# Hybrid SSD and attention step: scan filler in half items, one sample state per step, state products over 128 rows

## Chip, core and metric

The kernel runs on one core of one Trainium2 chip. The metric is the device time of one execution in microseconds (us), the median of several runs; lower is better. A profile is one further execution, recorded instruction by instruction.

## What is computed

One inference step of a two-layer decoder: 512 prompt tokens of one sequence and 8 sample sequences of 8 tokens each (576 tokens in all) share the weights. Layer 0 mixes tokens with a Mamba-2 state scan, layer 1 with sliding-window attention; each layer has a SwiGLU feed-forward block before and after its mixer. The part that matters here is the scan of layer 0, with 4 groups (G) of 8 heads (R) of 64 features (P) and a state of 128 (N):

```python
def ssd_mixer(h, conv_buf, h0, in_w, conv_w, conv_b, dt_bias, a_log, d_skip, norm_w, out_w):
    zxbcdt = h @ in_w
    ...
    xbc = jax.nn.silu(causal_dwconv(xpad, conv_w, conv_b, l))
    ...
    y, h_T = ssd_scan(xdt, dt * A, Bm, Cm, h0.reshape(bsz, SSM_GROUPS, SSM_HPG, SSM_HEAD_DIM, SSM_STATE))
    y = y + xs * d_skip.reshape(SSM_GROUPS, SSM_HPG, 1)
    yg = (y.reshape(bsz, l, SSM_D_INNER) * jax.nn.silu(z)).astype(jnp.float32).reshape(bsz, l, SSM_GROUPS, -1)
    yg = yg * lax.rsqrt(jnp.mean(yg * yg, axis=-1, keepdims=True) + RMS_EPS)
    ...
    return yn @ out_w, new_conv, new_h

# inside ssd_scan, per chunk of at most 128 tokens
    chunk_states = jnp.einsum('bclgn,bclgrp->bcgrpn', Bc, xc * decay_to_end[..., None])
    def step(hc, inp):
        s, a = inp
        return hc * a[..., None, None] + s, hc
    y_off = jnp.einsum('bclgn,cbgrpn->bclgrp', Cc, h_in) * jnp.exp(a_cs)[..., None]
```

For the 8 sample sequences there is one chunk of 8 tokens each: read the old state, add its part to y, and write old state times decay plus the product of B and the decayed inputs.

## The kernel before

Activations lie with features on the partitions and tokens along the free axis, 576 of them in two token halves `HALF`: 256 and 320 columns. A projection block is a product of a 1024 x 128 weight with all tokens. Weights and activations are each split into a high and a low part, and `gemm` (line 501) issues three matmuls for each of 8 slices of the contraction, 24 a half. `load_w` loads a block on SP's queue (tile `raw`, two buffers), ScalarE (ACT) casts the high part `whi`, VectorE (DVE) subtracts the low part `wlo`. All matmuls of `gemm` stand as `g<-...` in the rows.

The scan, in `ssd`, goes through the four groups in turn. `mix` is a generator: it issues a step of a group's scan and yields, nine times in a group: the transposes and products of B and C (`bcs`); four prompt chunks (`chunk`); the within-chunk part of the samples and `old(0)`; `new(0)`; `old(1)`; `new(1)`. Each `old` reads the states of four samples (tile `h0`, four buffers; it is `h` in the trace), loaded on SP's queue, into products `pos` with 32 weight columns each, and a transpose `yot`. Each `new` multiplies the four states by their decay on GpSimd (POOL, line 1013), forms two products `psts` for each sample (line 1009 with the high part `xh` of the inputs, line 1010 with the low part `xl`), adds on DVE (line 1016) and stores on ACT's queue. A state buffer of the first four samples is free for a load of the second four only when its store has landed. In the 64 rows of `xl` lie the low parts; `xh` has 128 rows.

Between steps the caller issues filling work from a list: projections of the next group (`nxt`, six items: B, C and four x blocks, each followed by a convolution on DVE, line 863), the gate projections of this group (`zs`, four) and the output projections of the group before (`outs`, four loads of two feature blocks). An item holds both token halves. After step k of nine, `nfill * (k + 1) / 9` items have been issued. After step `GK` = 6 the gated product of the first token half is issued (`gate_mul`: `y` times z, squares, sums in `gacc`), after the next step its sum over the features (`gate_sum`: a matmul `gsq` on TensorE). The last `NG` items lie between the parts of the gated norm, `GB` of them ahead of the second `gate_sum`, `GC` behind it.

The engines run their queues in order. The order inside a queue is set when the kernel is built: a scheduler takes instructions as its own estimate of times lets them become ready, so it differs from the order of the code.

Of the kernel before, what the change touches and what calls it, by code (L numbers as in the profile page):

```python
# [10 lines left out]
F32 = mybir.dt.float32  # L11
F32R = mybir.dt.float32r
AF = mybir.ActivationFunctionType
ALU = mybir.AluOpType
# [5 lines left out]
HALF = ((0, 256), (256, 320))  # L20
# [19 lines left out]
FS = 0  # L40
NPRE = 4
PSP = 512
NX = 1
NG = 2
GK = 6
GJ = 2
GA = 0
GB = 1
GC = 1
FP = (0, 2)  # L50
N2 = T // 2
# [7 lines left out]
def body(ctx: ExitStack, tc: tile.TileContext, A, O):  # L59
# [421 lines left out]
    def gemm(w, acts, n, w0=0):  # L481

        return gemms([w], acts, n, w0)[0]
# [21 lines left out]
    def hin_acts(hin, h):  # L505
        return [(hin[h][:, 0, k, :], hin[h][:, 1, k, :]) for k in range(8)]
# [10 lines left out]
    def run_in(hin, items, first, ex, pend, between=None, pre=()):  # L517

        bd = last.pop() if first and last else None
        base = len(mms)  # L520
        ws = [bd.nextw[i] if bd and i < len(bd.nextw) else pre[i][0] if i < len(pre) else
              load_w(src, 1024, ex if i >= WR else None)
              for i, (src, _) in enumerate(items[:first])]
        if bd:
            bd.update(1)
            bd.close()
        for h in (0, 1):
            if between and h:
                between()
            for i, (w, (_, use)) in enumerate(zip(ws, items)):  # L530
                if h == 0 and i < len(pre):
                    use(h, gemm_part(w, hin_acts(hin, h), HALF[h][1], range(4, 8), pre[i][1]))
                else:
                    use(h, gemm(w, hin_acts(hin, h), HALF[h][1]))
            if bd and h == 0:
                bd.place(1, base)
        for src, use in items[first:]:
            w = load_w(src, 1024)
            for h in (0, 1):
                use(h, gemm(w, hin_acts(hin, h), HALF[h][1]))  # L540
            pend.step()
# [227 lines left out]
    def ssd(l, hin, f, pend, bd):  # L769
        with ExitStack() as cx:  # L770
# [122 lines left out]
            def mix(g, d, y, sa, se, dtt, cd):  # L893
# [111 lines left out]
                def new(q, xh, xl):  # L1005

                    for b in range(q * 4, q * 4 + 4):
                        pst = ps_s.tile([128, 512], F32, tag="s", name="psts")
                        PE.matmul(out=pst, lhsT=bm[:, b, :], rhs=xh, start=True, stop=False)
                        PE.matmul(out=pst, lhsT=bm[0:64, b, :], rhs=xl, start=False, stop=True)  # L1010
                        h0 = h0s.pop(b)
                        hv = h0.rearrange("p (h q) -> p h q", q=64)
                        G.tensor_tensor(out=hv, in0=hv,
                                        in1=cd[:, g * 8:g * 8 + 8, 4 + b].unsqueeze(2).to_broadcast([128, 8, 64]),
                                        op=ALU.mult)
                        V.tensor_tensor(out=h0, in0=pst, in1=h0, op=ALU.add)
                        nc.scalar.dma_start(O["ssm_s"][g, :, b], h0)

                for i in range(5):
                    bcs(i)  # L1020
                yield
                h = None
                for i in range(4):
                    h = chunk(i, h)
                    yield
                skip(slice(0, NP))
                xd, pyv = within(4)
                old(0)
                yield
                xh = R2.tile([128, 512], F32R, tag="xdd", name="xh", bufs=2)  # L1030
                xl = R2.tile([64, 512], F32R, tag="xl", name="xl", bufs=1)
                S.copy(xh, xd)
                V.tensor_tensor(out=xl, in0=xd[0:64], in1=xh[0:64].bitcast(F32), op=ALU.subtract)
                new(0, xh, xl)
                yield
                old(1)
                yv = y[:, :, NP:T]
                V.tensor_tensor(out=yv, in0=pyv, in1=yv, op=ALU.add)
                skip(slice(NP, T))
                yield  # L1040
                new(1, xh, xl)
                yield

            def z_item(g, j, zt):

# [55 lines left out]

            R = tc.tile_pool(name="ssdr", bufs=1, reuse_waits="tile")
            Rcm, R = R, R.__enter__()
            def run1(item):
                run_in(hin, [item()], 0, None, pend)

            d, items = proj_items(0)
            v = R.tile([96, T], F32, tag="xs", name="dtv", bufs=6)
# [10 lines left out]
            for g in range(4):  # L1119
                last = g == 3  # L1120
                fill = []
                outs = [lambda ld=ld, yn=yn: run_out([ld], yn_acts(yn), f, g == 1) for ld in out_loads(g - 1)] if g else []
                zt, ynew = [], []

                def z_run(j):
# [6 lines left out]
                    run1(lambda: z_item(g, j, zt[j]))  # L1132

                zs = [lambda j=j: z_run(j) for j in range(4)]
                dn, nxt = proj_items(g + 1) if not last else (None, [])
                nxt = [lambda it=it: run1(it) for it in nxt]
                fill = zs + outs if last else nxt[:NX] + outs + zs + nxt[NX:]
                nfill = len(fill) - NG

                y = R.tile([128, 4, T], F32, tag="y", name="y", bufs=1)  # L1140
                steps = mix(g, d, y, *dd)
                done = 0
                for k, _ in enumerate(steps):
                    while done < nfill * (k + 1) / 9:
                        fill.pop(0)()
                        done += 1
                    if k == GK:
                        acc = gate_mul(0, y, zt)
                    if k == GK + 1:
                        r0 = gate_sum(0, acc)  # L1150
                fl = iter(fill)
                run = lambda c: [next(fl, lambda: None)() for _ in range(c)]
                acc = gate_mul(1, y, zt)
                ynew += [yn_alloc() for _ in range(4)]
                run(GA)
                gate_norm(0, g, y, bcast(r0, HALF[0][1]), ynew)
                run(GB)
                r1 = gate_sum(1, acc)
                run(GC)
                gate_norm(1, g, y, bcast(r1, HALF[1][1]), ynew)  # L1160
                run(len(fill))
                yn, d = ynew, dn
# [523 lines left out]
```

## Time and profile before

| what | value |
|---|---|
| time, median of 3 runs | 2581.92 us (2581.41 to 2588.04) |
| the profiled execution's own time | 2593.07 us |
| span of its profile, first to last instruction | 2591.0 us |
| TensorE (PE) matmul busy | 2493.8 us, 96% |
| VectorE busy | 1804.0 us, 70% |
| ScalarE busy | 1152.3 us, 44% |
| GpSimd busy | 202.8 us, 8% |
| mean granted TensorE clock | 0.977 |

The profiled execution took 11 us longer than the median. Busy times come from the record of each instruction; a matmul's end is modelled, so for TensorE the spacing of starts tells more than the busy share. In a timeline row the bracket at the end is the idle time of that engine just before the row, and what ended it. The scan runs from about 556 us to 995 us of the span. A 32-bit matmul that is not split stands as two records.

### The profile page before, as it was taken

Reading aid. Unit: us, or ns where it says so; the run is one execution under the profiler, and the core shown is the slowest. Engines: PE = TensorE matmul, PEld = TensorE weight load, DVE = VectorE, ACT = ScalarE, POOL = GpSimd, SP = SyncE. Lnnn points to the kernel's source line nnn. Section 1 sums busy time; section 2 is a strip of 40 time slices with the busy share of each in tenths; the row PEclk is TensorE's granted clock in tenths of the full one; section 3 lists DMA queues with packets and bytes.
Section 4 is the critical chain, followed back from the end, with each engine's and each line's share of the span. In section 5 each row is a group of like instructions: output and inputs, shape, how many; then the busy total and the mean of one; then the engine's idle time right before and its main releaser. Section 6 shows DMA issues by size and latency. Waiting matters only on the chain.

```text
span 2591.0 us, 45688 instructions
## 1 busy us (share of the span) xinstructions
PE 2493.8 (96%) x18247; PEld 2309.2 (89%) x18247; DVE 1804.0 (70%) x3415; ACT 1152.3 (44%) x2396; POOL 202.8 (8%) x338
## 2 busy tenths in 40 slices
PE   6999999989999999999999999999999998999997
PEld 5999998877989878899999999999899788999997
DVE  5576766887768686667767757675766756577685
ACT  4343434554645454334424534342454664343343
POOL 1000000123131312000000100000010001000001
PEclk8999999999999999899999999999999998999998
DMA  7344534244444342344333343443436123233222
GB/s 261 106 167 135 191 134 167 94 117 130 122 131 107 131 115 107 120 138 127 122 135 120 121 139 107 167 177 126 168 124 202 34 70 107 94 101 103 91 94 110
DMA packets 119499, 331.04 MB, mean 128 GB/s; under 512 B 17903, under 2 KB 39903, under 8 KB 108671
## 3 DMA queue, kind: packets, MB, share of 16 engines
q1 hardware_dynamic: 100535, 245.46, 29.3%
q10 hardware_dynamic: 18752, 82.68, 9.3%
q8 instruction: 143, 2.34, 0.4%
q14 instruction: 69, 0.57, 0.1%
HBM read 301.63 MB, written 29.67 MB: 128 GB/s over the span
## 4 chain that ended last, share of the span: by engine, by line
PE 80%; DVE 8%; DMA 4%; ACT 3%; issue 3%; POOL 1%; SPq 0%; DVEq 0%; ACTq 0%; POOLq 0%
PE g L501 40%; PE g L673 29%; PE adaps L164 2%; DMA w<-scr_a 1%; PE gram L343 1%; DVE wlo L472 1%; DVE acc L863 1%; DMA raw<-in_w_out 1%; PE po L1298 1%; DVE hin L439 1%; PE py L947 1%; PE ssq L234 1%; DVE pn L436 1%; PE rb L255 1%; DMA x<-x_dram 1%
## 5 line engine op out<-in xcount | busy, mean ns | idle before, releaser
L501 PE MATMUL g<-hin,whi 128*128 128x320 f32 (+1 forms) x2528 | 533.4, 304 | 1.8 <-DVE hin L439 1.8
L501 PE MATMUL g<-mid,whi 128*128 128x320 f32 (+1 forms) x2432 | 489.3, 296 | 0.0
L673 PE MATMUL g<-hin,whi 128*128 128x288 f32 x2176 | 436.2, 294 | 0.0
L501 PEld LDWEIGHTS g<-hin,whi 128*128 128x128 f32 x2528 | 418.6, 194 | 10.3 <-issue 6.6
L501 PE MATMUL g<-hin,wlo 128*128 128x320 f32 (+1 forms) x1264 | 388.1, 309 | 16.1 <-ACT sil L724 7.0
L501 PEld LDWEIGHTS g<-mid,whi 128*128 128x128 f32 x2432 | 390.7, 188 | 1.1
L501 PE MATMUL g<-mid,wlo 128*128 128x256 f32 (+1 forms) x1216 | 359.8, 297 | 2.4 <-ACT mid L685 2.2
L673 PEld LDWEIGHTS g<-hin,whi 128*128 128x128 f32 x2176 | 349.1, 188 | 0.0
L673 PE MATMUL g<-tcmb,whi 128*128 128x288 f32 x1632 | 327.2, 294 | 0.0
L673 PE MATMUL g<-hin,wlo 128*128 128x288 f32 x1088 | 324.2, 298 | 0.0
L469 ACT CAST whi<-raw 128x1024 fp32r<-128x1024 f32 (+2 forms) x209 | 188.0, 900 | 236.3 <-PE g L501 162.5
L472 DVE TENSOR_TENSOR wlo<-raw,whi 128x1024 fp32r<-128x1024 f32 (+3 forms) x209 | 216.4, 1038 | 85.7 <-ACT whi L469 84.7
L501 PEld LDWEIGHTS g<-hin,wlo 128*128 128x128 f32 x1264 | 244.3, 194 | 33.7 <-issue 11.0
L673 PEld LDWEIGHTS g<-tcmb,whi 128*128 128x128 f32 x1632 | 262.5, 189 | 0.0
L673 PE MATMUL g<-tcmb,wlo 128*128 128x288 f32 x816 | 245.5, 301 | 0.0
L501 PEld LDWEIGHTS g<-mid,wlo 128*128 128x128 f32 x1216 | 228.6, 188 | 7.1 <-ACT mid L685 4.6
L652 ACT CAST whi<-scmb 128x512 fp32r<-128x512 f32 (+1 forms) x204 | 154.3, 760 | 160.8 <-PE g L673 83.5
L673 PEld LDWEIGHTS g<-hin,wlo 128*128 128x128 f32 x1088 | 204.1, 188 | 23.9 <-issue 23.9
L566 DVE TENSOR_TENSOR f<-g,f 128x256 f32<-128x256 f32 (+1 forms) x240 | 108.6, 455 | 143.4 <-PE g L501 142.2
L648 DVE TENSOR_TENSOR wlo<-scmb,whi 128x512 fp32r<-128x512 f32 (+1 forms) x204 | 175.6, 863 | 36.1 <-ACT whi L652 35.2
L673 PEld LDWEIGHTS g<-tcmb,wlo 128*128 128x128 f32 x816 | 153.3, 188 | 25.1 <-DVE ur L648 19.7
L652 ACT CAST whi<-raw 128x512 fp32r<-128x512 f32 x136 | 84.7, 623 | 166.2 <-PE g L673 98.4
(299 smaller groups left out, 3898.9 us busy)
## 6 DMA issues: line engine op xcount, KB each, us to landing
adaw<-in_ada_w ACTq DMA_DIRECT2D x56, 1024.0 KB, 5.4
raw<-in_w_in SPq DMA_DIRECT2D x108, 512.0 KB, 3.5
rawu<-in_w_in SPq DMA_DIRECT2D x68, 512.0 KB, 4.5
raw<-in_w_out SPq DMA_DIRECT2D x64, 384.0 KB, 3.1
raw<-in_w_out SPq DMA_DIRECT2D x64, 320.0 KB, 3.0
raw<-in_w_ssm SPq DMA_DIRECT2D x40, 512.0 KB, 3.5
x_dram<-x SPq DMA_DIRECT2D x10, 1024.0 KB, 3.9
x<-x_dram SPq DMA_DIRECT2D x10, 1024.0 KB, 6.3
```

The source lines that it names most:

```text
L164: PE.matmul(out=pt[32 * j:32 * j + 32, :w], lhsT=cs[:, k, :], rhs=aw[:, j * w:j * w + w], start=(k == 0), stop=(k == 7))
L234: ins = PE.matmul(out=ps[:, c0 + i:c0 + i + 1], lhsT=acc[:, o:o + 128], rhs=ones[:, 0:1], start=True, stop=True)
L255: ins = PE.matmul(out=r[:, c:e], lhsT=mul(y[:, i:i + 1], [128, 128]), rhs=ident[:, 128 - (e - c):128], start=True, stop=True)
L343: ins = PE.matmul(out=out, lhsT=a, rhs=b, start=(o == i == 0), stop=(o == 7), skip_group_check=True)
L436: V.scalar_tensor_tensor(out=tm, in0=x_cur[h][:, k, :], scalar=mv["gs"][:, k, 0:1], in1=r[:, :256], op0=ALU.mult, op1=ALU.mult)
L469: S.copy(hi[:, :n], raw[:, :n])
L472: i = (V if early and c < PSP else eng or V).tensor_tensor(out=lo[:, c:e], in0=raw[:, c:e], in1=hi[:, c:e].bitcast(F32), op=ALU.subtract)
L501: mms.append(PE.matmul(out=p[:, :n], lhsT=wt[:, a:b], rhs=at, start=(k == j == 0), stop=(j == 2 and k == K - 1)))
L566: V.tensor_tensor(out=fs, in0=p, in1=fs, op=ALU.add)
L648: e.tensor_tensor(out=out, in0=a, in1=b, op=op)
L652: S.copy(w[0][:, c:c + n], src)
L673: mms.append(PE.matmul(out=p, lhsT=wt[:, o], rhs=x, start=(first and k == j == 0), stop=(k == 3 and j == 2), skip_group_check=True))
```

## The change

The filling list now holds pieces: a projection item is two pieces, one for each token half (`pieces`), and an output load is two pieces, one for each feature block with both halves (`out_pieces`). The counts double with them (`NX` 1 to 2, `NG` 2 to 4); `GB` goes from one item to three pieces, `GC` stays at one, now a piece. `mix` yields after each sample of `new`, with weights that add to 36; pieces are issued up to `nfill * k / 36`. The gated product of the first half follows at k = 28 and its sum at k = 32, the same places of `mix` as before. The low part `xl` now has 128 rows, of which the upper 64 are set to zero on DVE, and the second product of a state takes all 128 rows of `bm`.

```diff
-NX = 1
-NG = 2
-GK = 6
+NX = 2
+NG = 4
...
-GB = 1
+GB = 3
...
-                        PE.matmul(out=pst, lhsT=bm[0:64, b, :], rhs=xl, start=False, stop=True)
+                        PE.matmul(out=pst, lhsT=bm[:, b, :], rhs=xl, start=False, stop=True)
...
                         nc.scalar.dma_start(O["ssm_s"][g, :, b], h0)
+                        yield 1
...
-                xl = R2.tile([64, 512], F32R, tag="xl", name="xl", bufs=1)
+                xl = R2.tile([128, 512], F32R, tag="xl", name="xl", bufs=1)
+                V.memset(xl[64:128].bitcast(F32), 0.0)
                 S.copy(xh, xd)
-                V.tensor_tensor(out=xl, in0=xd[0:64], in1=xh[0:64].bitcast(F32), op=ALU.subtract)
-                new(0, xh, xl)
-                yield
+                V.tensor_tensor(out=xl[0:64], in0=xd[0:64], in1=xh[0:64].bitcast(F32), op=ALU.subtract)
+                yield from new(0, xh, xl)
...
+            def pieces(item):
+
+                got = {}
+
+                def half(h):
+                    if h == 0:
+                        src, got["use"] = item()
+                        got["w"] = load_w(src, 1024)
+                    got["use"](h, gemm(got["w"], hin_acts(hin, h), HALF[h][1]))
+                    if h:
+                        pend.step()
+
+                return [lambda h=h: half(h) for h in (0, 1)]
+
+            def out_pieces(ld, yn, first):
...
+                def one(i):
+                    if i == 0:
+                        got["w"] = load_w(src, n)
+                    o, w0 = os_[i]
+                    for h in (0, 1):
+                        p = gemm(got["w"], yn_acts(yn)(h), HALF[h][1], w0)
...
-                done = 0
-                for k, _ in enumerate(steps):
-                    while done < nfill * (k + 1) / 9:
+                done = k = 0
+                for part in steps:
+                    k += part
+                    while done < nfill * k / 36:
                         fill.pop(0)()
                         done += 1
-                    if k == GK:
+                    if k == 28:
                         acc = gate_mul(0, y, zt)
-                    if k == GK + 1:
+                    if k == 32:
                         r0 = gate_sum(0, acc)
```

The order moves in all four groups from the sample part of the first on. Three places follow, all in the second group (group 1), where the kernel before has its pattern of the middle groups. One removed line of constants makes the line numbers ahead of the inserted code smaller by one after the change.

TensorE, the first four state products of group 1, before (the number after `psts` tells one sample from the next; `g` is filling work):

```order
L1009 MATMUL psts_8040<-xh_8036,bm_7235 128x512
L1010 MATMUL psts_8040<-xl_8037,bm_7235 128x512
L1009 MATMUL psts_8046<-xh_8036,bm_7235 128x512
L1010 MATMUL psts_8046<-xl_8037,bm_7235 128x512
L1009 MATMUL psts_8052<-xh_8036,bm_7235 128x512
L1010 MATMUL psts_8052<-xl_8037,bm_7235 128x512
L501 MATMUL g_8071<-hin_5193,wlo_8068 128x256
...
L1009 MATMUL psts_8058<-xh_8036,bm_7235 128x512
L1010 MATMUL psts_8058<-xl_8037,bm_7235 128x512
```

The same place after:

```order
L1008 MATMUL psts_8042<-xh_8037,bm_7236 128x512
L1009 MATMUL psts_8042<-xl_8038,bm_7236 128x512
L500 MATMUL g_8055<-hin_5193,wlo_8052 128x256
...
L1008 MATMUL psts_8083<-xh_8037,bm_7236 128x512
L1009 MATMUL psts_8083<-xl_8038,bm_7236 128x512
L500 MATMUL g_8089<-hin_5193,wlo_8052 128x320
...
L1008 MATMUL psts_8117<-xh_8037,bm_7236 128x512
L1009 MATMUL psts_8117<-xl_8038,bm_7236 128x512
L1008 MATMUL psts_8123<-xh_8037,bm_7236 128x512
L1009 MATMUL psts_8123<-xl_8038,bm_7236 128x512
```

A whole token half of filling work (24 matmuls) now stands behind the first product pair and another behind the second.

TensorE, the four state reads of `old(1)` of group 1 up to the transpose `yot`, before:

```order
L994 MATMUL pos_8232<-h0_8233,C_6621 32x512
L994 MATMUL pos_8232<-h0_8235,C_6621 32x512
L994 MATMUL pos_8232<-h0_8237,C_6621 32x512
L994 MATMUL pos_8232<-h0_8239,C_6621 32x512
L501 MATMUL g_8266<-hin_5193,wlo_8263 128x256
...
L1000 MATMUL yot_8247<-c_ident_89,yo_8245 128x128 x4
```

and after:

```order
L993 MATMUL pos_8190<-h0_8191,C_6621 32x512
L993 MATMUL pos_8190<-h0_8193,C_6621 32x512
L500 MATMUL g_8216<-hin_5193,wlo_8135 128x320
...
L993 MATMUL pos_8190<-h0_8195,C_6621 32x512
L500 MATMUL g_8216<-hin_5193,wlo_8135 128x320
L500 MATMUL g_8216<-hin_5193,whi_8134 128x320 x2
...
L993 MATMUL pos_8190<-h0_8197,C_6621 32x512
L500 MATMUL g_8268<-hin_5193,wlo_8265 128x256
...
L999 MATMUL yot_8205<-c_ident_89,yo_8203 128x128 x4
```

The four reads stood together and are now a pair and two single ones, with filling work between; 24 filling matmuls stand between the fourth state product and the first read, where 92 stood.

DVE of group 1, from the convolution of C to the sums of squares of the first token half (`gacc`), which the matmul `gsq` reads; before:

```order
L863 SCALAR_TENSOR_TENSOR acc<-xpt,c_convw,acc 128x64
L1003 TENSOR_TENSOR y<-yot,y 128x4x32
L472 TENSOR_TENSOR wlo<-raw,whi 128x1024
L870 SCALAR_TENSOR_TENSOR C<-th,acc 128x320
L1038 TENSOR_TENSOR y<-py,y 128x4x64
L953 SCALAR_TENSOR_TENSOR y<-xs,c_dsk,y 128x64 x4
L1066 TENSOR_TENSOR gacc<-gacc,sq 128x256
L1060 SCALAR_TENSOR_TENSOR y<-y,z 128x320
```

and after:

```order
L862 SCALAR_TENSOR_TENSOR acc<-xpt,c_convw,acc 128x256 x3
L869 SCALAR_TENSOR_TENSOR C<-th,acc 128x256
L1065 TENSOR_TENSOR gacc<-gacc,sq 128x256 x2
L862 SCALAR_TENSOR_TENSOR acc<-xpt,c_convw,acc 128x256 x2
L862 SCALAR_TENSOR_TENSOR acc<-xpt,c_convw,acc 128x64
...
L1002 TENSOR_TENSOR y<-yot,y 128x4x32
```

The sums now stand ahead of the second half of C's convolution and of the work behind `yot`; before they stood behind both.

## Rows read from the trace of the kernel before

**Rows 1.** The page: TensorE's granted clock in 40 slices, and the chain.

```profile
PEclk8999999999999999899999999999999998999998
PE 80%; DVE 8%; DMA 4%; ACT 3%; issue 3%; POOL 1%; SPq 0%; DVEq 0%; ACTq 0%; POOLq 0%
```

**Rows 2.** TensorE's waits from 556 to 995 us: total, times, longest.

```profile
PE gsq L234 <- DVE gacc L1066: 7.5, 6, 2.8
PE py L947 <- DVE w L943: 3.1, 7, 1.1
```

**Rows 3.** Windows: PE, PEld, DVE, ACT, POOL busy, clock, DMA share, GB/s.

```profile
700.00:740.00 40.00, 40.00 (x291) 34.89 (x291) 22.90 (x38) 12.55 (x28) 6.30 (x7) 1.00 0.42 133
740.00:775.00 35.00, 32.22 (x205) 28.20 (x204) 27.81 (x58) 19.88 (x51) 13.43 (x27) 0.90 0.38 118
865.00:900.00 35.00, 32.22 (x192) 27.42 (x191) 25.55 (x53) 18.70 (x47) 11.72 (x24) 0.85 0.37 122
```

**Rows 4.** The state products' tile: duration min/median/max in ns, first and last start.

```profile
L1009 PE MATMUL psts<-xh,bm x32: 388/502/794, 610.8 to 984.9; 128*128 128x512 f32 x32
L1010 PE MATMUL psts<-xl,bm x32: 491/500/792, 611.1 to 985.3; 64*128 64x512 f32 x32
```

**Rows 5.** Timeline of weight loads, first four state products: start, length, idle before.

```profile
611.50 0.19 PEld L1009 LDWEIGHTS psts<-xh,bm 128*128 128x128 f32 x1 [0.24 <-issue]
611.93 0.18 PEld L1010 LDWEIGHTS psts<-xl,bm 64*128 64x128 f32 x1 [0.24 <-issue]
612.36 0.19 PEld L1009 LDWEIGHTS psts<-xh,bm 128*128 128x128 f32 x1 [0.24 <-issue]
```

**Rows 6.** Timeline of matmuls, filling work at full clock.

```profile
720.21 0.28 PE L501 MATMUL g<-hin,wlo 128*128 128x256 f32 x1
...
720.57 0.31 PE L501 MATMUL g<-hin,wlo 128*128 128x320 f32 x1
...
721.01 0.31 PE L501 MATMUL g<-hin,wlo 128*128 128x320 f32 x1
```

**Rows 7.** Timeline of matmuls, first gated sum of groups 1 and 2.

```profile
751.29 0.61 PE L234 MATMUL gsq<-c_ones,gacc 128*128 128x1 f32 x4 [2.78 <-DVE gacc L1066]
...
757.72 0.41 PE L501 MATMUL g<-hin,wlo 128*128 128x256 f32 x1
...
758.36 0.41 PE L501 MATMUL g<-hin,wlo 128*128 128x256 f32 x1
...
879.90 1.01 PE L234 MATMUL gsq<-c_ones,gacc 128*128 128x1 f32 x4 [2.78 <-DVE gacc L1066]
```

**Rows 8.** Timeline of DVE and POOL ahead of that sum.

```profile
741.60 5.10 DVE L863 SCALAR_TENSOR_TENSOR acc<-xpt,c_convw,acc 128x256 f32<-128x256 f32 x6 [1.13 <-ACT acc L860]
...
750.82 0.41 DVE L1066 TENSOR_TENSOR gacc<-gacc,sq 128x256 f32<-128x256 f32 x1
...
741.53 4.49 POOL L1013 TENSOR_TENSOR h<-h,cd 128x512 f32<-128x512 f32 x4 [0.26 <-PE pos L994]
```

**Rows 9.** Timeline of matmuls around state reads: four together, then a single one.

```profile
740.01 0.46 PE L501 MATMUL g<-hin,whi 128*128 128x320 f32 x2
...
741.40 0.39 PE L501 MATMUL g<-hin,wlo 128*128 128x256 f32 x1
...
973.18 0.28 PE L501 MATMUL g<-yn,whi 128*128 128x256 f32 x1
...
974.36 0.38 PE L501 MATMUL g<-yn,whi 128*128 128x256 f32 x1
```

**Rows 10.** State stores and loads (KB, us to landing), and a read that waits.

```profile
h<-in_h SPq DMA_DIRECT2D x32, 256.0 KB, 4.2
out_ssm_s<-h ACTq DMA_DIRECT2D x32, 256.0 KB, 2.1
...
621.94 1.05 PE L994 MATMUL pos<-h,C 128*32 128x512 f32 x2 [0.23 <-DMA h<-in_h]
```

**Rows 11.** The low part's tile: duration min/median/max in ns.

```profile
L1033 DVE TENSOR_TENSOR xl<-xdd,xh x4: 784/802/1204, 605.8 to 961.4; 64x512 fp32r<-64x512 f32 x4
```

More of the change, by code (lines that the diff above doesn't have):

```diff
@@ L1017, in new @@
                         nc.scalar.dma_start(O["ssm_s"][g, :, b], h0)
+                        yield 1
                 for i in range(5):
                     bcs(i)
-                yield
+                yield 4
                 h = None
@@ L1024, in mix @@
                     h = chunk(i, h)
-                    yield
+                    yield 4
                 skip(slice(0, NP))
@@ L1028, in mix @@
                 old(0)
-                yield
+                yield 4
                 xh = R2.tile([128, 512], F32R, tag="xdd", name="xh", bufs=2)
-                xl = R2.tile([64, 512], F32R, tag="xl", name="xl", bufs=1)
+                xl = R2.tile([128, 512], F32R, tag="xl", name="xl", bufs=1)
+                V.memset(xl[64:128].bitcast(F32), 0.0)
                 S.copy(xh, xd)
-                V.tensor_tensor(out=xl, in0=xd[0:64], in1=xh[0:64].bitcast(F32), op=ALU.subtract)
-                new(0, xh, xl)
-                yield
+                V.tensor_tensor(out=xl[0:64], in0=xd[0:64], in1=xh[0:64].bitcast(F32), op=ALU.subtract)
+                yield from new(0, xh, xl)
                 old(1)
@@ L1039, in mix @@
                 skip(slice(NP, T))
-                yield
-                new(1, xh, xl)
-                yield
+                yield 4
+                yield from new(1, xh, xl)
             def z_item(g, j, zt):
@@ L1103, in ssd @@
             Rcm, R = R, R.__enter__()
+            def pieces(item):
[9 more added lines that the diff above has]
+            def out_pieces(ld, yn, first):
+                src, n, os_ = ld
+                got = {}
+                def one(i):
[4 more added lines that the diff above has]
+                        p = gemm(got["w"], yn_acts(yn)(h), HALF[h][1], w0)
+                        if first:
+                            S.copy(f[h][:, o, :], p)
+                        else:
+                            V.tensor_tensor(out=f[h][:, o, :], in0=p, in1=f[h][:, o, :], op=ALU.add)
+                return [lambda i=i: one(i) for i in range(len(os_))]
             def run1(item):
-                run_in(hin, [item()], 0, None, pend)
+                for piece in pieces(item):
+                    piece()
             d, items = proj_items(0)
@@ L1121, in ssd, with z_make @@
                 fill = []
-                outs = [lambda ld=ld, yn=yn: run_out([ld], yn_acts(yn), f, g == 1) for ld in out_loads(g - 1)] if g else []
+                outs = [p for ld in out_loads(g - 1) for p in out_pieces(ld, yn, g == 1)] if g else []
                 zt, ynew = [], []
-                def z_run(j):
+                def z_make(j):
                     if not last:
@@ L1131, in z_run @@
                                   R.tile([128, 608], F32, tag="C", name="z", bufs=2)[:, 0:T])
-                    run1(lambda: z_item(g, j, zt[j]))
-                zs = [lambda j=j: z_run(j) for j in range(4)]
+                    return z_item(g, j, zt[j])
+                zs = [p for j in range(4) for p in pieces(lambda j=j: z_make(j))]
                 dn, nxt = proj_items(g + 1) if not last else (None, [])
-                nxt = [lambda it=it: run1(it) for it in nxt]
+                nxt = [p for it in nxt for p in pieces(it)]
                 fill = zs + outs if last else nxt[:NX] + outs + zs + nxt[NX:]
```

## The prediction

> **What bounds the kernel now.** I read the chain of work first: 80% of the span is TensorE, most of it filling work and feed-forward products, so a microsecond taken from TensorE's queue is one of the span unless something else is late there [rows 1]. The slices of the granted clock show two dips in the middle of the run, in the scan [rows 1]. Next I read TensorE's waits over the scan alone: the largest is `gsq`, the sum of the gated squares, waiting for `gacc` on DVE, 7.5 us in six waits, the longest 2.8; the next, the within-chunk products waiting for their weights, is 3.1 us in seven [rows 2]. Then three windows: from 700 to 740 us TensorE has no idle time and a clock of 1.00; in the two windows that hold the first `gsq` of groups 1 and 2 it idles 2.8 us each, and the clock falls to 0.90 and 0.85 of full over 35 us [rows 3]. Last the state products, 32 pairs of 512 columns, whose single durations near 500 ns say little; their spacing says more [rows 4, 5]. So the stage is bound by TensorE's spacing of instructions, with two short places where DVE is late.
>
> **State products over 128 rows.** The weight loads of a pair start 0.43 us apart, 611.50, 611.93 and 612.36, and each begins 0.24 us after the one before it ended: none is drawn ahead under a running matmul, neither the 64-row load behind the 128-row one nor the reverse [rows 5]. Filling work, all of it on 128 rows, goes otherwise: three matmuls of 256 columns take 0.36 us, three of 320 take 0.44, so 0.12 and 0.147 each, less than a weight load (0.19) and so with the load hidden [rows 6, 5]. 64 columns more cost 0.027, so 512 columns should cost 0.147 + 3 x 0.027 = 0.23. A pair falls from 0.86 to 0.46 us; 32 pairs give 32 x 0.40 = **12.8 us**. The bounds are 0, if the spacing has nothing to do with the rows, and 13.8, if time goes with columns alone (512 x 0.12 / 256 = 0.21 x 2, so 0.43 a pair). I take the value by the filling work, which is the same engine and form. Spread between pieces, the pairs lose nothing, since no change of rows is left there.
>
> The Trainium skill, page "TensorE: Matmul & The Clock Gate", section "The mechanism" of Part 3, speaks against this gain: it says that a weight load overlaps a running matmul only where the two use different row groups, and full rows share all of theirs. By that rule the pair stays at 0.86. Filling work at 0.12 us a matmul with loads of 0.19 disagrees with it [rows 6, 5].
>
> **The wait at the first gated sum.** In groups 1 and 2 `gsq` waits 2.78 us each time [rows 7]. On DVE `gacc` stands behind the second half of C's convolution, of which six steps took 5.10 us while POOL worked on four states for 4.49, and comes at 750.82 [rows 8]. In the new order `gacc` stands ahead of those steps and of the work behind `yot`, while `gsq` on TensorE still has a C half, an x item and the reads of `old(1)` ahead of it. POOL's part of the sum now comes behind two of the four states instead of behind four. So the waits should go: 2 x 2.78 = **5.6 us**.
>
> Behind each of these waits the clock stands at 1.2 instead of 2.4 GHz for a while: 0.10 and 0.15 of 35 us are missing, 8.75 us of clock, or 17.5 us at the low level [rows 3]. There three filling matmuls of 256 columns take 0.64 us against 0.36, so 0.28 / 0.64 = 0.44 of the time is lost: 17.5 x 0.44 = **7.7 us**. What TensorE did before the fall was to idle 2.78 us; without that I expect no fall.
>
> **What it costs.** The state reads are split. Four together cost 741.40 - 740.01 - 2 x 0.147 = 1.10 us of filling work; a single one costs 974.36 - 973.18 - 0.12 = 1.06 [rows 9, 6]. One read costs as much as four side by side. In groups 1 and 2 one such event becomes three, in group 3 three become four, in group 0 four stay four, since there a wait had already parted the first two [rows 10]: five events more at 1.08, **+5.4 us**. If the new pairs don't run side by side it is seven events, 7.6; the lower bound is four, 4.3.
>
> These reads also come sooner after the state products that free their buffers. The second product of group 1 now has 24 x 0.147 + 2 x 0.46 + 24 x 0.12 = 7.3 us of work between it and its read. The way through is the product (0.46), the sum on DVE (under 0.8, the time of the low part's subtraction), the store (2.1) and the load (4.2): 7.6 us by medians [rows 10, 11]. Before, 92 filling matmuls stood there, some 12 us, and one such wait of 0.23 was left in group 0 [rows 10]. SP's queue now holds the loads behind up to one more weight load. Between 0 and 2.8 us a group (the longest wait of the scan, rows 2), so 0 to 11 us; near the low end by the medians: **+2.5 us**.
>
> DVE did 27.8 us of work in the 35 us that now shrink [rows 3]: TensorE's share becomes about 35 - 2.8 (wait) - 3.1 (clock, 0.44 of 7) - 1.6 (four pairs) + 2.2 (two events) = 30 us, so DVE is at 93%. What is late next is the second gated sum of the same group, whose waits are the small ones among the six, 7.5 - 5.6 = 1.9 us in four [rows 2, 7]. I put **+2 us** on it; bounds 0 and 5.6, all of the wait back. The new zeros of 64 x 512 on DVE stand ahead of that sum; they cost at most what the subtraction of the same size takes, 0.80, four times, 3.2 us, and at least nothing [rows 11]; DVE still has a tenth free, so **+0.5**. Smaller pieces also shift the cover of the chunk steps, where 3.1 us of waits stand [rows 2]; they could go or double, and I count zero.
>
> **The sum.** -12.8 - 5.6 - 7.7 + 5.4 + 2.5 + 2 + 0.5 = -15.7 us on the profiled execution's 2593.07, 0.61%. That execution is 11 us above the median of the runs; the same share of 2581.92 gives **2566 us**.
>
> **The rivals.**
> *The wait moves on.* DVE has the same work in less time; if it is the bound, TensorE meets the second `gsq` as early as it leaves the first, waits some 2.8 us there and the clock falls again. Then the 5.6 and 7.7 are gone, and so is the 2: -12.8 + 5.4 + 2.5 + 0.5 = -4.4 us, 2577.5. For it: 93%, and small waits that already stand there [rows 2, 3]. Against it: more than two items of filling work lie between the two sums, and DVE gets the first `gacc` done earlier. 0.17.
> *Full rows gain nothing.* The spacing of the pairs stays: -15.7 + 12.8 = -2.9, 2579. Only the rule cited above is for it; the filling work's spacing is against [rows 6]. 0.07.
> *Slower: reads wait for their states.* If the way from product to read is 10 us rather than 7.6, TensorE idles 2.8 us in each group and the clock falls as it does now: 4 x (2.78 + 7.7 / 2) = 26.5 us in place of the 2.5, so +8.3, 2590. It decides at some 10 us. For it: in group 0 the second product's weights were loaded at 611.50 and a read waited until 621.94 [rows 5, 10]. Against it: there the four sums came late on DVE and the loads came in two batches. 0.08.
> *Better.* None of the guessed costs (2.5, 2, 0.5) comes, the pairs save 13.8, the clock's loss was the whole 8.75, and the small waits at `gsq`, 1.9, go as well: -13.8 - 5.6 - 8.75 + 5.4 - 1.9 = -24.7, 2557. 0.12.
>
> **How the numbers follow.** The forecast, 2560 to 2573, has 0.56. Within 0.3% of the median, about what a measurement of this kernel can tell from no change, means 2574.2 to 2589.7. Faster: the forecast but for 0.02 of it, the better case, and a third of the first rival, 0.72. Same: the rest of the first rival, the second, 0.20. Slower: the third, 0.08. The range must take in the better case and most of the first rival: 2556 to 2578.
>
> **What will show it.** Weight loads of the state products 0.23 us apart with no idle time before them; no wait of 2 us at `gsq` and a clock of 1.00 in the middle groups; three read events in groups 1 and 2, with waits under 1 us on the state loads. The forecast is wrong if the clock still dips in the scan, at the second `gsq` or at a read, or if the pairs keep their 0.43.

## The result and the profile after

The changed kernel takes **2571.48 us** against 2587.35, medians of six runs each: a ratio of **0.9939**, 95% interval 0.9920 to 0.9958, so 0.61% faster. The forecast was 2566.0 on a base of 2581.92, a ratio of 0.9938. The profiled execution took 2572.65 us (before 2593.07), its mean granted clock is 0.983 (before 0.977).

The page's slices of the granted clock, and the shares of the chain (before: [rows 1]):

```profile
PEclk9999999999999999899999999999999998999998
PE 79%; DVE 8%; DMA 4%; ACT 3%; issue 3%; POOL 1%; SPq 0%; DVEq 0%; ACTq 0%; POOLq 0%
```

Only the first slice differs. A slice is 65 us long, and the one 8 in the middle is the 17th, from some 1030 us on and so behind the scan: the prediction took this row for dips in the scan, which only the windows show [rows 3].

TensorE's waits from 556 to 995 us (before: [rows 2]; the rows of before that do not stand there add 3.7 us):

```profile
PE py L946 <- DVE xdt L928: 3.4, 4, 1.7
PE pos L993 <- DMA h<-in_h: 3.4, 4, 1.3
PE py L946 <- DVE w L942: 2.9, 4, 1.0
PE pst L969 <- DVE xdd L928: 2.6, 2, 1.6
PE gsq L233 <- DVE gacc L1065: 1.2, 2, 0.6
PE pos L993 <- DVE f L1131: 0.9, 1, 0.9
PE psts L1009 <- DVE xl L1034: 0.4, 1, 0.4
```

`py` and `pst` are products of the chunk steps; `pos` are the reads of the states. The read whose wait of 0.9 us is put down to `f` got its state 0.13 us before it started (landed at 958.08, read at 958.21), so I count it with the waits for states. `gsq` fell from 7.5 us to 1.2, but the sum of all waits is 14.8 us where it was 14.3: the time came back at the reads of the states (0.2 to 4.3) and in the chunk steps.

The windows (before: [rows 3]); the clock is at full level in all three:

```profile
700.00:740.00 40.00, 39.23 (x282) 33.81 (x283) 23.51 (x37) 12.83 (x29) 8.87 (x10) 1.00 0.40 131
740.00:775.00 35.00, 34.41 (x245) 31.98 (x244) 29.58 (x67) 23.50 (x57) 11.31 (x28) 1.00 0.41 132
865.00:900.00 35.00, 33.59 (x237) 31.16 (x238) 28.66 (x65) 22.57 (x55) 11.24 (x27) 1.00 0.41 138
```

Weight loads of state products (before: [rows 5]): starts 0.23 us apart, no idle time ahead of them.

```profile
612.93 0.19 PEld L1009 LDWEIGHTS psts<-xl,bm 128*128 128x128 f32 x1
613.16 0.19 PEld L1008 LDWEIGHTS psts<-xh,bm 128*128 128x128 f32 x1
613.39 0.19 PEld L1009 LDWEIGHTS psts<-xl,bm 128*128 128x128 f32 x1
```

Matmuls of group 1, the first gated sum (before: [rows 7]), and one of group 2, a read (before: [rows 9, 10]):

```profile
749.41 0.50 PE L233 MATMUL gsq<-c_ones,gacc 128*128 128x1 f32 x4
...
865.82 1.04 PE L993 MATMUL pos<-h,C 128*32 128x512 f32 x2 [1.33 <-DMA h<-in_h]
```

The reads over the scan, busy time, mean ns, idle time; the first row is of before, the second of after:

```profile
L994 PE MATMUL pos<-h,C 128*32 128x512 f32 x64 | 14.3, 605 | 0.2 <-DMA h<-in_h 0.2
```

```profile
L993 PE MATMUL pos<-h,C 128*32 128x512 f32 x64 | 21.0, 604 | 4.4 <-DMA h<-in_h 3.4 <-DVE f L1131 0.9
```

State loads and stores (before: [rows 10]): the store's median is 3.5 us now, and was 2.1.

```profile
h<-in_h SPq DMA_DIRECT2D x32, 256.0 KB, 4.2
out_ssm_s<-h ACTq DMA_DIRECT2D x32, 256.0 KB, 3.5
```

Behind the scan, the first `gram` (of the norm that follows), before and then after:

```profile
1018.13 0.97 PE L343 MATMUL gram<-f,x 128*128 128x128 f32 x6 [2.41 <-ACT f L328]
```

```profile
1004.75 0.97 PE L342 MATMUL gram<-f,x 128*128 128x128 f32 x6 [1.19 <-ACT f L327]
```

Without that wait the scan ends at 1015.72 before and 1003.56 after, 12.2 us sooner; the span is 20.2 us shorter. So 8.0 us of the difference between these two executions lie behind the scan, past the part that the change reorders: 1.2 are the wait on `f`, and in the 90 us from `gram` on the mean clock is 0.92 where it was 0.87:

```profile
1018.13:1108.13 90.00, 83.59 (x534) 79.78 (x535) 55.76 (x108) 36.17 (x72) 5.18 (x14) 0.87 0.30 100
```

```profile
1004.75:1094.75 90.00, 82.53 (x556) 78.61 (x557) 57.84 (x111) 36.91 (x74) 6.69 (x15) 0.92 0.30 100
```

4.5 us of missing clock are 9 us at the low level, of which 0.44 is lost: 4.0 us. That leaves 2.8 us, no more than single executions scatter by: the runs of the kernel before span 10 us. The 8.0 us are not all the change's: the profiled execution of the kernel before is slower than all six runs timed here, and takes 1575.2 us from the end of the scan on, where the four other kernels with whole items (below) take 1564.3 to 1570.2 and this one takes 1567.3. By the medians 15.9 us were gained, 3.7 more than the scan shows.

### The profile page after: what moved, and what is told of

It is laid out like the page before. It is cut to its first block, busy times and chain, and to the rows that moved or that the text cites. A ratio compares the mean times of both kernels' runs of the same rounds, so it can differ in the third digit from the quotient of the medians.

```text
span 2570.8 us, 45698 instructions
## 1 busy us (share of the span) xinstructions
PE 2474.9 (96%) x18247; PEld 2299.4 (89%) x18247; DVE 1800.1 (70%) x3419; ACT 1153.6 (45%) x2396; POOL 197.1 (8%) x338
## 4 chain that ended last, share of the span: by engine, by line
PE 79%; DVE 8%; DMA 4%; ACT 3%; issue 3%; POOL 1%; SPq 0%; DVEq 0%; ACTq 0%; POOLq 0%
PE g L500 40%; PE g L672 29%; PE adaps L163 2%; DMA w<-scr_a 1%; PE gram L342 1%; DVE wlo L471 1%; DMA raw<-in_w_out 1%; PE po L1331 1%; DMA h<-in_h 1%; PE py L946 1%; DVE pn L435 1%; DVE acc L862 1%; DVE st L348 1%; PE rb L254 1%; PE ssq L233 1%
## 5 line engine op out<-in xcount | busy, mean ns | idle before, releaser
L500 PE MATMUL g<-hin,whi 128*128 128x320 f32 (+1 forms) x2528 | 527.9, 302 | 1.8 <-DVE hin L438 1.8
L500 PE MATMUL g<-hin,wlo 128*128 128x320 f32 (+1 forms) x1264 | 384.8, 306 | 15.8 <-ACT sil L723 7.2
L500 PEld LDWEIGHTS g<-hin,wlo 128*128 128x128 f32 x1264 | 241.4, 192 | 36.0 <-issue 13.7
L565 DVE TENSOR_TENSOR f<-g,f 128x256 f32<-128x256 f32 (+1 forms) x208 | 94.2, 455 | 132.9 <-PE g L500 131.9
```

The lines of the kernel that those rows point to most:

```text
L500: mms.append(PE.matmul(out=p[:, :n], lhsT=wt[:, a:b], rhs=at, start=(k == j == 0), stop=(j == 2 and k == K - 1)))
L565: V.tensor_tensor(out=fs, in0=p, in1=fs, op=ALU.add)
```

## The experiments

All times are ratios to the kernel before, which ran beside each of them on the same chip; kernels of different rounds are compared through these ratios. Gains in us are worked out on the medians of before (2584 to 2588). "Scan" is the start of the first `gram` against 1018.13, from one execution each; early in the scan, the first matmul `cbp` starts between 545.8 and 552.0 us in the fourteen traces, so 2 or 3 us of scan say little.

**128 rows alone.** The kernel before with this part of the change:

```diff
-                        PE.matmul(out=pst, lhsT=bm[0:64, b, :], rhs=xl, start=False, stop=True)
+                        PE.matmul(out=pst, lhsT=bm[:, b, :], rhs=xl, start=False, stop=True)
...
-                xl = R2.tile([64, 512], F32R, tag="xl", name="xl", bufs=1)
+                xl = R2.tile([128, 512], F32R, tag="xl", name="xl", bufs=1)
+                V.memset(xl[64:128].bitcast(F32), 0.0)
```

> The kernel before with one part of the change: the low part xl over 128 rows (upper 64 zero), so that both products of a state use full rows; the filling work and its order stay as they were. My theory: the spacing of the 32 pairs falls from 0.86 to 0.46 us, 12.8 us off the scan; the two waits of 2.78 us at the first gated sum of groups 1 and 2 and the fall of the clock behind them stay, since DVE is as late as before. Ratio to the kernel before 0.995 (0.994 to 0.9965). Rival, full rows gain nothing: weight loads stay 0.43 us apart, ratio 1.000. Second rival, the gain is given back: the pairs are faster but the waits at the gated sum grow by what the pairs save in groups 1 and 2 (some 3 us each), ratio 0.9975.

Measured 0.9947 (0.9927 to 0.9967), 13.7 us; the scan is 14.3 shorter. The waits at `gsq` stayed, 7.5 us in six, as expected. The clock did not do what I expected. A window of group 2, and the gated sum in it:

```profile
865.00:900.00 35.00, 31.57 (x232) 30.46 (x231) 31.14 (x71) 22.50 (x56) 12.83 (x25) 1.00 0.39 129
```

```profile
872.23 0.61 PE L234 MATMUL gsq<-c_ones,gacc 128*128 128x1 f32 x4 [2.78 <-DVE gacc L1067]
```

The same wait of 2.78 us, and the clock stays at 1.00; in group 1 it is 0.95 (before: 0.90 and 0.85). So the wait alone does not bring it down.

**The change without the 128 rows** (the same diff the other way, on the changed kernel).

> The changed kernel with one part undone: xl on 64 rows again, the pieces and the steps of one sample kept. My theory: weight loads of a pair are 0.43 us apart again and single pairs between pieces lose at least as much, so 12.8 us slower than the changed kernel; the waits at the first gated sum stay away and the clock stays at 1.00 in the scan. Against the kernel before that leaves about 3 us, ratio 0.999 (0.997 to 1.000). Rival, the order alone carries the gain (5.6 + 7.7 of the prediction with nothing given back): ratio 0.995. Rival, full rows matter less when pairs stand alone between pieces: within 4 us of the changed kernel.

Measured 0.9971 (0.9959 to 0.9982), 7.5 us faster than before, at the edge of my range, and 8.3 slower than the changed kernel. The scan is 3.4 us shorter than before, near the 3 I expected. The clock is 1.00 in both middle windows:

```profile
740.00:775.00 35.00, 34.50 (x227) 29.84 (x224) 28.51 (x62) 21.30 (x53) 15.73 (x30) 1.00 0.46 150
865.00:900.00 35.00, 34.85 (x222) 28.98 (x221) 27.48 (x60) 20.28 (x51) 11.06 (x25) 1.00 0.48 157
```

The two halves give 13.7 and 7.5 us alone and 15.8 together, 5.4 us less than their sum. The three intervals leave some 8 us open there (an estimate from their half widths of 5.2, 3.0 and 4.9 us), so the times alone do not show this loss; the scans, 14.3, 3.4 and 13.4 us shorter, show one of some 4 us. Reads wait 0.5 us for states here and 4.3 in the changed kernel, where the products come faster.

**The gated product earlier, nothing else.** In the kernel before:

```diff
                     while done < nfill * (k + 1) / 9:
+                        if k == GK and done + 1 >= nfill * (k + 1) / 9:
+                            acc = gate_mul(0, y, zt)
                         fill.pop(0)()
                         done += 1
-                    if k == GK:
-                        acc = gate_mul(0, y, zt)
```

> The kernel before with only the gated product of the first token half issued one filling item earlier; whole items, four samples a step, 64 rows. It tells whether the early place of the sums on DVE alone takes the wait and the clock's fall away. My theory: the two waits of 2.78 us go and the clock stays at 1.00 in groups 1 and 2, 13 us off, ratio 0.995. Rival, the wait moves on: DVE has the same work, so the second gated sum or the chunk steps wait instead, and 0 to 3 us are left, ratio 0.999 to 1.000.

Measured 0.9971 (0.9957 to 0.9986), 7.5 us, between the two expectations. The waits of 2.78 us at `gsq` are gone, but a new wait stands two product pairs behind it:

```profile
752.08 0.50 PE L1009 MATMUL psts<-xh,bm 128*128 128x512 f32 x1 [1.67 <-ACT gv L1075]
```

The pool that takes these products has three PSUM buffers; the third state product needs the one that `gsq` filled and `gv`, on ScalarE, has to read. The clock is 0.95 in both windows. The scan is 6.9 us shorter: all waits together fell from 14.3 to 11.9 us, and 0.15 of 35 us of clock came back, which by the prediction's working is some 4.6 us.

**128 rows and the earlier product together** (both diffs on the kernel before).

> The kernel before with 128 rows and with the gated product one filling item earlier, so two edits that were worth 13.7 and 7.5 us alone; whole items, four samples a step. If they add, ratio 0.992. They overlap in one thing: with 128 rows alone the clock's fall was already small. Theory: 128 rows keep the clock up, the earlier sums take away the waits of 2.78 us and a new wait of some 2 us for the third product behind the gated sum comes (it needs the PSUM buffer that the sum holds), ratio 0.9925 (0.9915 to 0.994), so better than the changed kernel without any pieces. Rival: the pieces are needed, ratio 0.9945 as with 128 rows alone.

Measured 0.9941 (0.9923 to 0.9958), an interval that holds both the theory's 0.9925 and the rival's 0.9945 (128 rows alone give 0.9947), so the times do not decide. The scan is 3.7 us shorter than with 128 rows alone and 4.6 shorter than in the changed kernel, so in the scan the pieces are not needed. As the theory said, the wait was exchanged, `gsq` 7.5 to 2.0 us and `psts` 0.8 to 4.9:

```profile
PE psts L1009 <- ACT gv L1076: 4.9, 2, 2.5
...
PE gsq L234 <- DVE gacc L1067: 2.0, 2, 1.0
```

**Four samples a step.** The changed kernel, but:

```diff
                         nc.scalar.dma_start(O["ssm_s"][g, :, b], h0)
-                        yield 1
+                    yield 4
```

> The changed kernel, but a step holds four samples again (one yield after the four, with the weight of all), so that the reads of the states stand four together; half pieces and 128 rows kept. My theory: the split of the reads (in the changed kernel three events in place of one in groups 1 and 2, about 1.08 us each) and the 4.3 us of waits of the reads for their states go, so some 8 us faster than the changed kernel, ratio to the kernel before 0.990. Rival: four state products in a row wait for DVE's sums and for the buffers of PSUM, as they did not with pieces between them, and the gain is 0 to 2 us. Second rival: four states' POOL work comes at once again, DVE's convolution is slow beside it, the wait of 2 us or more at the first gated sum comes back with the clock's fall, and it is slower than the changed kernel, ratio 0.997.

Measured **0.9903** (0.9885 to 0.9921), 25 us; 2559.85 us is the lowest median of all. Reads and waits:

```profile
L993 PE MATMUL pos<-h,C 128*32 128x512 f32 x64 | 14.8, 604 | 1.1 <-DMA h<-in_h 1.1
```

```profile
PE psts L1008 <- ACT gv L1074: 3.9, 2, 2.1
...
PE pos L993 <- DMA h<-in_h: 1.1, 2, 0.7
```

The reads cost 6.2 us less than in the changed kernel and wait 3.2 less, against a new wait of 3.9 at `gv`; the scan is 9.5 us shorter than in the changed kernel, and the second rival's wait at `gsq` did not come. The step of one sample costs more than it brings.

**Two samples a step** (a `yield 2` after every second sample).

> The changed kernel with two samples a step. The reads of the second four still come in three events in groups 1 and 2, as in the changed kernel, but filling work stands between the second and the third state product, so that the third does not wait for the PSUM buffer of the gated sum (3.9 us in two waits with four samples a step). Theory: the split reads cost about 1.05 us an event and the reads wait for states as in the changed kernel, so 0.9925 to 0.994, between the changed kernel and four samples a step. Rival: only a step of one sample is harmful, 0.990 or better.

Measured 0.9917 (0.9899 to 0.9936): in between, as far as the intervals tell, and just under my range. No wait at `gv`, but 3.0 us at `gsq` in two waits; reads 18.6 us, waits for states 1.7.

**Five state buffers.** The changed kernel with `HB = 5`.

> The changed kernel with five state buffers instead of four; nothing else differs. In the changed kernel the second four reads of a group wait 4.3 us in all for states (five waits of 0.2 to 1.3 us) and are split in three events in groups 1 and 2. Theory: the waits come from the way through a buffer, from product to store to load; with one buffer more they shrink to under 1.5 us and the reads group three and one, so 4 to 6 us faster than the changed kernel, ratio to the kernel before 0.992 (0.991 to 0.993). Rival: the waits for states are only the place where another lateness shows (DVE's sums, the chunk steps); the reads no longer wait, but the time turns up at other waits, ratio 0.994 as the changed kernel.

Measured 0.9909 (0.9891 to 0.9927), 23.5 us, at the edge of my range, but not by the waits: those for states are still 3.5 us. The busy time of the reads fell:

```profile
L993 PE MATMUL pos<-h,C 128*32 128x512 f32 x64 | 17.5, 604 | 3.6 <-DMA h<-in_h 3.5
```

That is 3.5 us of the 5.5 by which the scan is shorter than in the changed kernel. What was bought is fewer events of reads.

**Further on from four samples a step.** Three kernels: with five buffers, with the first gated sum issued behind the four products of the second half (`if k == 36` ahead of the filling loop in place of `if k == 32` behind it), and with both.

> The changed kernel with four samples a step and five state buffers. With four samples a step the reads already stand four together and wait 1.1 us for states, so the fifth buffer has little left to give. If its gain in the changed kernel (some 7 us) came through fewer events of reads, it gives 0 to 2 us here, ratio 0.9895 to 0.9905. If it came through an earlier state for the work behind the reads, it gives 4 us or more, ratio 0.988 or better.

> The changed kernel with four samples a step, and the first gated sum issued behind the four state products of the second half instead of ahead of them. With four samples a step the third product waited 3.9 us in two waits for the PSUM buffer of that sum, whose reader on ScalarE comes some 4 us after it. Theory: these waits go and nothing takes their place, ratio 0.9888 (0.988 to 0.9895). Rival: the gated norm of the first half comes that much later and TensorE waits for it, or the next step waits for the buffer instead; ratio 0.990 to 0.992.

> Both edits on the kernel with four samples a step: the gated sum behind the products and five state buffers. If both theories hold, 0.987 to 0.989, the fastest so far; if the waits only move on, 0.990 as with four samples a step alone.

Measured 0.9920 (0.9903 to 0.9936), 0.9910 (0.9893 to 0.9928) and 0.9935 (0.9918 to 0.9953). None is shown to be better than four samples a step (0.9903); the first two cannot be told from it, and the third is slower, beyond both of the outcomes that I gave. My theory of the second, that nothing takes the place of the waits, fell. With the sum behind the products, the wait on `gv` is gone, and the fourth product waits for the buffer that DVE has not yet emptied:

```profile
PE psts L1008 <- DVE h L1015: 5.2, 3, 2.7
```

With five buffers alone the waits on `gv` and `gsq` grow to 5.3 and 3.0 us. DVE and ScalarE get through the same work no sooner; a stall taken from one place comes back at the next.

**Four samples a step and 64 rows**, a test of the clock.

> The changed kernel with four samples a step and 64 rows of xl, so the run with four samples a step but for the rows. With 128 rows its third product waited about 2 us in groups 1 and 2 and the clock stayed at 1.00. Theory: the clock falls where a wait of 2 us meets the slow pairs of 64 rows (0.43 us a product, engine idle 0.24 of it), and not where it meets pairs of 128 rows; so here the clock falls to half for some 4 us behind that wait in both groups, and the kernel is 12.8 + 3.5 us slower than with 128 rows, ratio 0.9966. Rival: the fall goes with waits of over 2.1 us alone; no fall here, ratio 0.9953.

Measured 0.9964 (0.9949 to 0.9979), 15.8 us slower than with 128 rows. The waits at the third product are only 1.42 and 0.49 us here, shorter than with 128 rows (2.08 and 1.84), and yet the clock falls, in both groups:

```profile
740.00:775.00 35.00, 33.58 (x217) 30.64 (x216) 27.75 (x62) 20.68 (x53) 13.84 (x28) 0.90 0.38 126
865.00:900.00 35.00, 34.51 (x221) 29.93 (x220) 28.04 (x61) 20.48 (x53) 14.66 (x29) 0.95 0.38 129
```

**Half as many changes of rows.** The kernel before, with the products of every second sample in reverse order (high, low, low, high):

```diff
+                        parts = [(bm[:, b, :], xh), (bm[0:64, b, :], xl)]
+                        if b % 2:
+                            parts.reverse()
+                        for i, (lh, rh) in enumerate(parts):
+                            PE.matmul(out=pst, lhsT=lh, rhs=rh, start=i == 0, stop=i == 1)
```

> The kernel before with xl on 64 rows as it is, but the two products of every second sample in reverse order, so that two products of 64 rows follow each other and then two of 128: the number of changes between the row counts halves, from about 64 to 32, nothing else. Theory: the lost time goes with each change of the row count, so loads behind one of the same rows start 0.21 to 0.23 us after it, and those behind a change 0.43 as before; 32 x 0.2 = 6.4 us off, ratio 0.9975 (0.996 to 0.9985). Rival: every load of or behind a 64-row product is slow, whatever stands ahead of it; all spacings stay 0.43, ratio 1.000.

Measured 0.9981 (0.9968 to 0.9995), 4.9 us. Weight loads, where x2 is two loads of the same rows:

```profile
609.34 0.29 PEld L1013 LDWEIGHTS psts<-xl,bm 64*128 64x128 f32 x2 [0.28 <-issue]
609.99 0.30 PEld L1013 LDWEIGHTS psts<-xh,bm 128*128 128x128 f32 x2 [0.36 <-issue]
610.66 0.29 PEld L1013 LDWEIGHTS psts<-xl,bm 64*128 64x128 f32 x2 [0.37 <-issue]
```

Two products take 0.65 to 0.67 us, where two changes took 0.86 and none takes 0.46: the 0.43 of a change and the 0.23 of none add to 0.66. Within a pair of the same rows the second load starts 0.11 us after the first, behind a change 0.55 after the one before; matmuls start 0.33 apart, and two of 64 rows side by side are as fast as two of 128. The time went with the change of the row count, about 0.2 us each, not with the 64 rows. The waits of 2.78 us stayed, and the clock is 0.85 in both windows, no better than before. The scan is only 1.7 us shorter in this execution: its waits are 17.0 us in all where they were 14.3, and the fall in group 1 is longer.

## Why the prediction was right

**State products, 12.8 us: right.** The spacing is the 0.23 us that filling work gave, and the three comparisons that differ in the rows alone gave 13.7 (kernel before), 8.3 (changed kernel) and 15.8 us (four samples), each give or take some 5 us or more, so the times do not tell them apart. The scans differ by 14.3, 10.0 and 16.1 us, and that spread fits what stands around the pairs: waits for states take some back (0.5 against 4.3 us), and the clock gives some more. The rival that full rows gain nothing is out. The rule of the Trainium skill that stood for it ("TensorE: Matmul & The Clock Gate", "The mechanism") does not hold for these pairs: a load behind the same rows starts under the running matmul, and the one that does not is the load behind another row count.

**The wait at the first gated sum, 5.6 us: the step held, the gain did not last.** All waits at `gsq` lost 6.3 us, the second gated sum among them: its +2 did not come (1.9 us of small waits became 1.2). But the waits of the scan as a whole grew by 0.5. The run with the product moved alone shows what such a move is worth: the next user of the PSUM buffer waits. The prediction had DVE at 93% behind this place; in the windows after it is busy 29.6 and 28.7 of 35 us, 85% and 82%.

Why `gacc` was late before, [rows 8] show but the prediction did not price. In the kernel before, three convolution steps of 128x256 just ahead, with POOL idle, took 1.53 us:

```profile
738.03 1.53 DVE L863 SCALAR_TENSOR_TENSOR acc<-xpt,c_convw,acc 128x256 f32<-128x256 f32 x3 [1.23 <-ACT acc L860]
```

The six steps of the second half (three of 256 columns, three of 64) took 5.10 us. Beside POOL's decay of the states single steps took 1.28 and 1.08 us, behind it 0.47 and 0.27. At the short lengths the six would take some 2.3 us (an estimate), 2.8 less, as much as `gsq` waits. So POOL's work beside them accounts for about the whole wait. No run took that work away, so this is a reading of the trace.

**The clock, 7.7 us: right in size, its cause only seen in part.** I tied the fall to the wait of 2.78 us alone. The granted clock of the two windows in all fourteen kernels, one execution each:

| kernel | wait, groups 1 and 2, us | changes of rows | clock |
|---|---|---|---|
| before | 2.78, 2.78 at `gsq` | yes | 0.90, 0.85 |
| half as many changes | 2.78, 2.78 at `gsq` | half | 0.85, 0.85 |
| gated product earlier | 1.67, 1.67 at third product | yes | 0.95, 0.95 |
| four samples, 64 rows | 1.42, 0.49 at third product | yes | 0.90, 0.95 |
| change without 128 rows | 0.96, 0.96 at second `gsq`, pairs apart | yes | 1.00, 1.00 |
| the change | 0.77, 1.33 at a read | no | 1.00, 1.00 |
| the change with five buffers | 0.87, 1.33 at a read | no | 1.00, 1.00 |
| 128 rows alone | 2.78, 2.78 at `gsq` | no | 0.95, 1.00 |
| 128 rows and earlier | 2.44, 2.45 at third product | no | 0.95, 1.00 |
| four samples a step | 2.08, 1.84 at third product | no | 1.00, 1.00 |
| four samples and five buffers | 2.63, 2.64 at third product | no | 1.00, 0.95 |
| four samples, sum behind the products | 2.15, 2.67 at fourth product | no | 0.95, 0.95 |
| four samples and both | 2.99, 2.98 at fourth product | no | 0.95, 1.00 |
| two samples a step | 1.27, 1.70 at second `gsq` | no | 1.00, 0.95 |

Where no wait stands beside the pairs there is no fall, even with changes of rows (the change without 128 rows). Beside a wait, 0.05 to 0.15 of a window is missing with changes of rows, and 0 to 0.05 with full rows, at waits as long or longer. So the wait and the gaps between the pairs' loads seem to work together, and each part of the change removes much of the fall alone: it may be counted only once. That they do is a reading, not shown: halving the changes left the clock no higher. And four falls in the scan lie outside the two windows, each just behind a wait: with full rows behind 1.90 us (four samples and five buffers) and 1.82 us (four samples and both) in group 0; and, far from the state products of the samples, behind a chunk step's wait of 1.93 us (two samples a step) and 2.17 us (four samples, 64 rows). Which of the two weighs more, and why the same wait gives 0.95 in one group and 1.00 in the other, stays open. Counting the clock once, and the waits for states, would account for the parts not adding, as far as they do not.

**Splitting the reads, +5.4 us: too low.** The reads' busy time rose by 6.7. In groups 1 and 2 one event became four, not three, because the pair that I saw in the order was parted by a wait for a state (0.77 us in group 1; in group 2 the second state landed at 860.12, 1.1 us behind the first read's start): seven events more, the upper bound that the prediction named (7.6).

**Waits for states, +2.5 us: too low.** They rose by 4.1. The term that was mis-sized is the store: 3.5 us to landing in place of 2.1, so the way from product to read is 0.46 + 0.68 (the sum) + 3.5 + 4.2 = 8.8 us by medians against the 7.3 that cover it. In group 1 the trace has the second product at 726.20, its sum's end at 727.67, a store of 4.12 us and a load of 3.73 that lands at 735.60, so 9.4 us; TensorE gets to its read at 734.87 and waits 0.77. Why the stores take longer was not tried. Five waits of 0.2 to 1.3 us, no fall of the clock: the slower rival's mechanism was there, short of its price.

**Chunk steps, 0 us within 3.1: near the upper bound.** `py` and `pst` together went from 6.4 to 8.9 us, +2.5. **Zeros of xl, +0.5:** four of 0.49 us on DVE, and one wait of 0.4 where 0.2 stood.

With these sizes the scan's sum is -12.8 - 6.3 - 7.7 + 6.7 + 4.1 + 2.5 + 0.2 = -13.3, measured -12.2. So the forecast was some 3 us too high for the scan. That the timed 15.9 us agree with the forecast 15.7 to within 0.2 is luck: costs set too low were made up by a gain behind the scan that the prediction did not have, and the interval of the measurement reaches 5 us to either side.

**What was not foreseen** is that gain. In all nine kernels with half pieces the first `gram` waits 1.2 us, in all five with whole items 2.4. The clock of the 90 us behind it is less clear: 0.85 to 0.89 with whole items, and with pieces 0.91 or 0.92 but for two (0.87 and 0.89). From the end of the scan to the last instruction the five with whole items take 1564.3 to 1575.2 us, on the mean 1568.7, the nine with pieces 1559.0 to 1571.1, on the mean 1564.7. So some 4 us are likely, with much overlap, and only the 1.2 at `gram` stand in every trace. Why pieces help there was not tried.

## What to carry to other kernels

Price a row count that alternates between neighbouring matmuls at the spacing of weight loads, not at the length of matmuls: padding to full rows, or putting products of like rows side by side, can be worth more than moving waits about. Before splitting work finely, look for neighbours that are cheap only while they stand together, as the state reads here. When an engine is late, compare its steps with the same steps elsewhere in the trace: here VectorE's were over twice as long while POOL worked. And when a wait is moved, ask who next needs the buffer it held, and count a fall of the clock once, however many edits would prevent it.

## What the runs showed of the hardware

Products of 512 columns that alternate between 64 and 128 rows start 0.43 us apart, products of 128 rows alone 0.23, and with a change at every second one 0.33, all at full clock. One state read of 32 weight columns occupies TensorE for 1.05 us, and four of them side by side 1.06. VectorE's convolution step of 128x256 took 1.28 us beside POOL's decay of the states and 0.48 without it. The granted clock stayed at 1.00 through a wait of 2.78 us (128 rows alone, group 2), and fell behind one of 0.49 us with products that change rows around it (four samples, 64 rows, group 2).
